# Modulation weight blocks loaded through GpSimd's queue instead of SyncE's, in a two-layer hybrid decoder

## The chip, the cores and the metric

The kernel runs on one core of one Trainium2 chip. A core has five engines with a queue of instructions each: TensorE (PE in the profile, its weight loads PEld), VectorE (DVE), ScalarE (ACT), GpSimd (POOL) and SyncE (SP). SyncE computes nothing; it issues DMAs. GpSimd computes and can issue DMAs too. Each queue is worked off in order: an instruction that waits holds up all that is behind it in its own queue. The metric is device time in microseconds (us) of one execution.

## The reference

Two layers over a residual stream of 1024 positions by 1024 channels, all float32. Each layer is:

```python
mod = c_act @ ada_w[l] + ada_b[l]            # c_act = silu(c): one row of 1024, ada_w[l]: 1024 x 6144
shift_m, scale_m, gate_m, shift_f, scale_f, gate_f = split(mod, 6)
h = rms_norm(x, g_pre_mix[l]) * (1 + scale_m) + shift_m
q, k, v, u = split(h @ w_in[l] + b_in[l])    # 512, 128, 128, 512 columns
attn = window_attention(rotary(q), rotary(k), v, sinks[l])   # window 128, 8 heads, 2 key heads
pool = pool_mixer(u, pool_w[l], pool_scale[l])
x = x + gate_m * rms_norm(concat(attn, pool) @ w_out[l], g_post_mix[l])
h = rms_norm(x, g_pre_ffn[l]) * (1 + scale_f) + shift_f
x = x + gate_f * rms_norm((silu(h @ w_gate[l]) * (h @ w_up[l])) @ w_down[l], g_post_ffn[l])
```

The change concerns the first line, the modulation: a product of one row with a matrix of 1024 x 6144 in each layer, 24 MB of weights that are read once and used for a single row.

## The kernel before

**The large products.** The sequence is worked in two halves of 512 positions. Every float32 product is made of three passes on TensorE: each operand is split into a high part (`hi`, written by ScalarE, L215) and a low part (`lo`, the rest, written by VectorE, L216), and `mm3` multiplies high by high (L255), high by low (L258) and low by high (L259). Weights arrive in `raw` (L225, issued by SyncE), are split, and are used at once. So TensorE depends at each step of a product on a DMA, on ScalarE and on VectorE.

**The modulation.** It is not done on TensorE as a matrix product. `ada_sum` takes blocks of 512 columns. Of a block it loads the eight pieces of 128 x 512 (256 KB each) one after another into the tile `ar` (L297), and VectorE multiplies each by a column of `c_act` and adds it into `ada` (L287 for the first piece, L289 for the seven others). `ar` has two buffers, so a piece can only be loaded once the sum of the piece two places earlier has freed its buffer. What is left in `ada` is one partial sum per partition; TensorE adds them up over the partitions with a few small matmuls (in `ada_pair`, `ada_gate` and `ada_columns`). `ada_pair` gives scale and shift, `ada_gate` a gate row, `ada_columns` scale and shift of the next layer's attention.

There are 20 such blocks, 160 loads. Eight blocks belong to each layer: two for the gate of attention, four for scale and shift of channel mixing and two for the gate of channel mixing. Four more, worked in layer 0's channel mixing, are scale and shift of layer 1's attention. (Layer 0's own shift and scale of attention are loaded in another way at the start and are not touched.)

**The order of the work.** The program is written as Python generators that are stepped against each other: `run(stream, steps, (other, n))` steps a main stream and lets others keep pace. The blocks of the modulation are a side stream (`side`). The stage in which it runs densest is this one, in each layer:

```python
run(out0, 2 * KD, (side, 4 * ADA), (att, 16))
```

`out0` is the output projection of half 0 (16 steps, `natural_proj`), `att` is the attention of half 1, and `side` works up to four blocks of the modulation meanwhile. A sum of the modulation is also tied behind the last split before it (`after(ins, recent["split"])`), so that it comes after that on VectorE.

From this program a scheduler makes the fixed order of each engine's queue. It weighs instructions by its own estimates of durations, those of the DMAs by the engine that issues them among them. So an edit of the issuing engine can also move instructions in queues that the edit doesn't name.

**What else stands in GpSimd's queue.** Set-up at the start, the zero fill of the value tiles of attention (`vz`, L752 and L760), the left margin of the pooling tiles (`uT`, L723 and L728, `halo`, L725) and the zeroed keys ahead of block 0 (`sa`, L782). One DMA is issued by GpSimd already: the load of the positions (L187).

**What else uses `ar`.** The rows of a gate (L441 and L442, stored by L448), the sums of the up projection (L1015) and the residual (L583), all issued by SyncE.

Of the kernel before, what the change touches and what calls it, by code (L numbers as in the profile page):

```python
# [65 lines left out]
def hybrid_decoder_kernel(  # L66
# [22 lines left out]
    nc = tc.nc  # L89
# [25 lines left out]
    def t_(tag, shape, dt=F32):  # L115
        if tag in SMALL:
            return small.tile(shape, dt, tag=tag, name=tag, bufs=SMALL[tag])
        if tag in SHARED:
            return sb.tile(shape, dt, tag=tag, name=tag, bufs=SHARED[tag])
        return now["pool"].tile(shape, dt, tag=tag, name=tag, bufs=REGIONS[now["name"]][tag])  # L120
# [92 lines left out]
    def split(hi, lo, src):  # L213

        nc.scalar.activation(hi, src, AF.Copy)  # L215
        recent["split"] = nc.vector.tensor_sub(lo, src, hi.bitcast(F32))  # L216
# [13 lines left out]
    def after(ins, prev):  # L230
        tc.add_manual_dep(
            ins.ins, prev.ins.name,
            mybir.DependencyInfo(mybir.DependencyClass.NoSync, mybir.DependencyReason.DATA),
            reason="order on the same engine",
        )
# [40 lines left out]
    def ada_sum(l, n0, got, whole=False):  # L276

        src = ada_w[l].rearrange("(p j) n -> p j n", j=KD)
        acc, ws = None, []
        for j in range(0, KD + 2, 2):
            for i, w in enumerate(ws, j - 2):
                if i == 0:
                    acc = t_("ada", [P, 512])
                    ins = nc.vector.tensor_scalar(acc, w, c_act[:, 0:1], None, op0=ALU.mult)  # L287
                else:
                    ins = nc.vector.scalar_tensor_tensor(  # L289
                        acc, w, c_act[:, i : i + 1], acc, op0=ALU.mult, op1=ALU.add  # L290
                    )
                after(ins, recent["split"])
            ws = []
            if j < KD:
                for i in (j, j + 1):
                    w = t_("ar", [P, 512])
                    nc.sync.dma_start(w, src[:, i, n0 : n0 + 512])  # L297
                    ws.append(w)
                yield
        if whole:  # L300
            got.append(acc)
        else:
            got += [t_("ph", [P, 512], F32R), t_("ph", [P, 512], F32R)]
            split(*got, acc)
        yield
# [156 lines left out]
    def ada_stream(jobs):  # L462

        for l, n0, close, *whole in jobs:
            got = []
            yield from ada_sum(l, n0, got, *whole)
            close(*got)
# [1105 lines left out]
```

## Time and profile before

| | |
|---|---|
| Time, median of 3 runs | 1915.66 us (1914.08 to 1919.38) |
| Profiled execution, its own time | 1912.51 us |
| Span from first to last instruction of it | 1910.7 us |
| TensorE busy | 1866.3 us (98%) |
| VectorE busy | 1545.1 us (81%) |
| ScalarE busy | 950.5 us (50%) |
| GpSimd busy | 26.8 us (1%) |
| Data moved by DMA | 341.86 MB, 179 GB/s over the span |
| of it by queue q1 (hardware_dynamic) | 340.17 MB |
| of it by queue q0 (software_dynamic) | under 0.01 MB, 32 packets |

The layers follow one another: attention and pooling of layer 0 to about 300 us, its channel mixing to about 950 us, layer 1's attention from about 985 to about 1250 us, then its channel mixing to the end. A row of a busy table gives, for a stretch of time, the busy time of each engine and in brackets the count of instructions, then the granted clock of TensorE as a share, the busy share of the DMA engines and GB/s. A row of a group gives the line in the code, the engine, the operation, the tiles written and read, and the count. A row of waits reads: who waited, for whom, how many us in total, how many times, the longest. "SPq" is SyncE's queue. The time of TensorE's matmuls is modelled and they overlap, so its busy share says less than the count of matmuls and the weight loads in a stretch.

### The profile page before, as it was taken

The page shows a single profiled execution, that of the slowest core. Times are in us where ns is not written, and L with a number is a line of the kernel's source. Part 1 is how long each engine was busy: PE and PEld are TensorE (multiplying, and loading weights), DVE is VectorE, ACT ScalarE, POOL GpSimd, SP SyncE. Part 2 cuts the span into 40 slices and gives each one's busy share as a digit, 9 for nine tenths or more (in the row PEclk, how much of TensorE's full clock was granted, in tenths as well). Part 3 has the DMA queues.
Part 4 walks back from the last instruction along what each step waited for, and adds up shares of the span by engine and source line. Part 5 has one row for each costly group of instructions (what it writes and reads, how often), then busy time and mean ns, then how long its engine had stood idle before and what let it go on. Part 6 is the DMA issues. An engine that isn't in the chain of part 4 may idle for free.

```text
span 1910.7 us, 26084 instructions
## 1 busy us (share of the span) xinstructions
PE 1866.3 (98%) x8978; PEld 1539.2 (81%) x8978; DVE 1545.1 (81%) x2898; ACT 950.5 (50%) x1789; POOL 26.8 (1%) x84
## 2 busy tenths in 40 slices
PE   6999999999999999999999989999999999999997
PEld 4887788888888888888888868888888887888886
DVE  5999886668898888788879998846889888877687
ACT  4876795653222223445548667845622222244452
POOL 1000000000000000000000000000000000000000
PEclk9999999999999999999999999999999999999999
DMA  9355563555655665944554464536654565574342
GB/s 324 115 155 153 163 226 122 186 177 183 204 179 189 208 207 178 323 137 145 183 168 128 133 183 165 177 110 208 215 188 150 198 209 202 197 252 150 115 152 102
DMA packets 227428, 341.86 MB, mean 179 GB/s; under 512 B 16952, under 2 KB 124360, under 8 KB 227296
## 3 DMA queue, kind: packets, MB, share of 16 engines
q1 hardware_dynamic: 227152, 340.17, 54.2%
q8 instruction: 70, 1.15, 0.2%
q14 instruction: 62, 0.51, 0.1%
q0 software_dynamic: 32, 0.00, 0.0%
q10 hardware_dynamic: 112, 0.04, 0.0%
HBM read 267.25 MB, written 72.89 MB: 178 GB/s over the span
## 4 chain that ended last, share of the span: by engine, by line
PE 79%; DVE 11%; DMA 5%; ACT 3%; issue 1%; SPq 0%; DVEq 0%; ACTq 0%
PE acc L255 24%; PE acc L258 24%; PE acc L259 24%; DMA ar<-in_ada_w_dram 2%; DVE lo L216 2%; DVE ada L289 2%; PE msc L851 1%; PE msc L519 1%; ACT hi L215 1%; DMA raw<-in_w_up_dram 1%; PE pv L255 1%; DVE ph L216 1%; DMA ar<-x 1%; DVE sb L816 1%; PE pv L258 1%
## 5 line engine op out<-in xcount | busy, mean ns | idle before, releaser
L215 ACT ACTIVATE hi<-raw 128x1024 fp32r<-128x1024 f32 (+1 forms) x388 | 332.4, 869 | 365.8 <-PE acc L258 196.2
L216 DVE TENSOR_TENSOR lo<-raw,hi 128x1024 fp32r<-128x1024 f32 (+1 forms) x388 | 380.0, 986 | 123.6 <-ACT hi L215 122.8
L255 PE MATMUL acc<-t,hi 128*128 128x512 f32 x704 | 274.6, 390 | 1.5 <-ACT hi L215 1.5
L258 PE MATMUL acc<-t,hi 128*128 128x512 f32 x704 | 274.0, 389 | 0.0
L259 PE MATMUL acc<-t,lo 128*128 128x512 f32 x704 | 271.9, 389 | 0.0
L255 PE MATMUL acc<-bh,hi 128*128 128x512 f32 x520 | 202.8, 390 | 0.0
L259 PE MATMUL acc<-bh,lo 128*128 128x512 f32 x520 | 202.4, 389 | 0.0
L255 PE MATMUL acc<-hT,hi 128*128 128x512 f32 x480 | 189.7, 395 | 0.6 <-DVE fn L638 0.6
L258 PE MATMUL acc<-hT,hi 128*128 128x512 f32 x480 | 188.4, 392 | 0.0
L259 PE MATMUL acc<-hT,lo 128*128 128x512 f32 x480 | 187.7, 392 | 0.0
L1107 DVE TENSOR_TENSOR fn<-acc,fn 128x512 f32<-128x512 f32 x220 | 150.2, 683 | 37.4 <-PE acc L259 37.4
L255 PEld LDWEIGHTS acc<-t,hi 128*128 128x128 f32 x704 | 132.2, 188 | 30.8 <-ACT hi L215 3.9
L259 PEld LDWEIGHTS acc<-t,lo 128*128 128x128 f32 x704 | 132.2, 188 | 29.0 <-DVE lo L216 1.5
L258 PEld LDWEIGHTS acc<-t,hi 128*128 128x128 f32 x704 | 132.2, 188 | 27.2
L258 PE MATMUL acc<-ph,hi 128*128 128x512 f32 x320 | 124.6, 389 | 0.0
L1043 ACT ACTIVATE fn<-fn 128x512 f32<-128x512 f32 x44 | 27.8, 633 | 180.3 <-DVE fn L1107 180.3
L289 DVE SCALAR_TENSOR_TENSOR ada<-ar,c_act,ada 128x512 f32<-128x512 f32 x140 | 104.6, 747 | 12.0 <-DMA ar<-in_ada_w_dram 11.0
L259 PEld LDWEIGHTS acc<-bh,lo 128*128 128x128 f32 x520 | 97.6, 188 | 20.4
L255 PEld LDWEIGHTS acc<-bh,hi 128*128 128x128 f32 x520 | 97.6, 188 | 20.0
L255 PEld LDWEIGHTS acc<-hT,hi 128*128 128x128 f32 x480 | 90.2, 188 | 18.9 <-DVE fn L638 1.4
L259 PEld LDWEIGHTS acc<-hT,lo 128*128 128x128 f32 x480 | 90.1, 188 | 18.2
L255 PE MATMUL acc<-hi 128*128 128x512 f32 x256 | 101.1, 400 | 2.8 <-DVE fn L638 1.6
(315 smaller groups left out, 3834.6 us busy)
## 6 DMA issues: line engine op xcount, KB each, us to landing
ar<-in_ada_w_dram SPq DMA_DIRECT2D x160, 256.0 KB
raw<-in_w_gate_dram SPq DMA_DIRECT2D x44, 512.0 KB
raw<-in_w_up_dram SPq DMA_DIRECT2D x44, 512.0 KB
raw<-in_w_in_dram SPq DMA_DIRECT2D x80, 256.0 KB
raw<-keeps SPq DMA_DIRECT2D x40, 512.0 KB
keeps<-fn SPq DMA_DIRECT2D x66, 256.0 KB
two_b<-in_w_down_dram SPq DMA_DIRECT2D x30, 512.0 KB
raw<-keepa SPq DMA_DIRECT2D x25, 512.0 KB
```

Source lines behind the costliest of these rows:

```text
L215: nc.scalar.activation(hi, src, AF.Copy)
L216: recent["split"] = nc.vector.tensor_sub(lo, src, hi.bitcast(F32))
L255: ins = nc.tensor.matmul(dst, lh, rh, start=first, stop=False)
L258: nc.tensor.matmul(dst, lh, rl, start=False, stop=False)
L259: return nc.tensor.matmul(dst, ll, rh, start=False, stop=last)
L289: ins = nc.vector.scalar_tensor_tensor(acc, w, c_act[:, i : i + 1], acc, op0=ALU.mult, op1=ALU.add)
L519: ins = nc.tensor.transpose(bank[:, t * P : (t + 1) * P], src[t], ident)
L816: nc.vector.tensor_tensor_reduce(out=s[:, ii, :], in0=bank[:, ii * 2 * P : (ii + 1) * 2 * P], in1=mask[:, min(blk, 1), :], scale=SCALE, sc ...
L851: nc.tensor.transpose(bank[:, i * P : (i + 1) * P], s[:, ii, ck * P : (ck + 1) * P], ident)
L1043: nc.scalar.activation(g, g, AF.Silu)
L1107: nc.vector.tensor_add(halves_of(dst)[m], bank, halves_of(src)[m])
```

## The change

One word of code: the 160 loads of `ada_sum` are issued by GpSimd.

```diff
@@ -294,7 +294,7 @@
             if j < KD:
                 for i in (j, j + 1):
                     w = t_("ar", [P, 512])
-                    nc.sync.dma_start(w, src[:, i, n0 : n0 + 512])
+                    nc.gpsimd.dma_start(w, src[:, i, n0 : n0 + 512])
                     ws.append(w)
                 yield
```

Shape, count, buffers and users of the loads stay as they are. The queues do not. SyncE's queue during the output projection of layer 0, before: weight loads of the projection (L225) and modulation loads (L297) alternate.

```order
L225 DMA raw<-in_w_out_dram 64x512 x6
L297 DMA ar<-in_ada_w_dram 128x512 x8
L225 DMA raw<-in_w_out_dram 64x512
L297 DMA ar<-in_ada_w_dram 128x512
L225 DMA raw<-in_w_out_dram 64x512
L297 DMA ar<-in_ada_w_dram 128x512
L225 DMA raw<-in_w_out_dram 128x512 x2
L297 DMA ar<-in_ada_w_dram 128x512
L225 DMA raw<-in_w_out_dram 128x512
L297 DMA ar<-in_ada_w_dram 128x512 x3
```

The same place in SyncE's queue with the change:

```order
L448 DMA gate<-ar 1x512
L457 DMA G<-gate 128x1024
L225 DMA raw<-in_w_out_dram 128x512
L225 DMA raw<-in_w_out_dram 64x512 x8
L225 DMA raw<-in_w_out_dram 128x512 x4
L225 DMA raw<-in_w_out_dram 64x512 x8
L225 DMA raw<-in_w_in_dram 128x512 x2
L546 DMA cfa<-in_x_dram 128x1024 x2
```

The weight loads of the projection now follow each other without a modulation load between them.

GpSimd's queue from the first part of attention to the end of the attention of layer 0, with the change (before, it held the same casts and copies and no L297):

```order
L297 DMA ar<-in_ada_w_dram 128x512 x7
L752 CAST vz<-vz_zero 128x64 x2
L297 DMA ar<-in_ada_w_dram 128x512 x4
L752 CAST vz<-vz_zero 128x64 x2
L297 DMA ar<-in_ada_w_dram 128x512 x4
L752 CAST vz<-vz_zero 128x64 x2
L297 DMA ar<-in_ada_w_dram 128x512 x20
L728 COPY uT<-halo 128x16
L297 DMA ar<-in_ada_w_dram 128x512 x4
L752 CAST vz<-vz_zero 128x64 x4
```

The zero fills of `vz` and the margin copy of `uT` now stand between loads that wait for a buffer.

VectorE's queue early in the output projection of layer 0, a piece of the difference (L289 are the sums of the modulation, L216 splits, L816 scores, L795 a split of queries):

```order
-L289 SCALAR_TENSOR_TENSOR ada<-ar,c_act,ada 128x512
 L216 TENSOR_TENSOR uT<-cfa,hi 128x512
-L216 TENSOR_TENSOR lo<-raw,hi 128x512
-L816 ISA sb,st<-msc,mask 128x256
-L816 ISA st 128x1
-L289 SCALAR_TENSOR_TENSOR ada<-ar,c_act,ada 128x512
-L816 ISA sb,st<-msc,mask 128x256
-L816 ISA st 128x1
+L289 SCALAR_TENSOR_TENSOR ada<-ar,c_act,ada 128x512
+L216 TENSOR_TENSOR lo<-raw,hi 128x512
 L216 TENSOR_TENSOR uT<-cfa,hi 128x512
 L289 SCALAR_TENSOR_TENSOR ada<-ar,c_act,ada 128x512
```

A sum that stood ahead of a split now stands behind it, and the scores between two sums have gone elsewhere; the number of instructions between the first and the last sum of the stage stays nearly the same.

## The prediction

> **What bounds the kernel now.** I read the page's busy shares first, then TensorE by stretches, then the chain of waits inside the weak stretches.
>
> ```profile
> span 1910.7 us, 26084 instructions
> PE 1866.3 (98%) x8978; PEld 1539.2 (81%) x8978; DVE 1545.1 (81%) x2898; ACT 950.5 (50%) x1789; POOL 26.8 (1%) x84
> ```
>
> TensorE seems full, but its busy time is modelled. The table of busy time by stretch says more, by the count of matmuls (the x behind PE) and by the weight loads (PEld).
>
> ```profile
> core 0: us, PE busy (x) PEld busy (x) DVE busy (x) ACT busy (x) POOL busy (x), PEclk, DMA share, GB/s
> 150.00:175.00 25.00, 21.84 (x115) 17.06 (x115) 24.17 (x63) 15.75 (x37) 0.42 (x2) 1.00 0.54 148
> 175.00:200.00 25.00, 23.47 (x118) 18.15 (x117) 23.57 (x61) 14.92 (x37) 0.00 (x0) 1.00 0.72 210
> 600.00:625.00 25.00, 25.00 (x112) 20.72 (x111) 21.90 (x30) 7.10 (x8) 0.00 (x0) 1.00 0.57 196
> 1100.00:1125.00 25.00, 22.26 (x110) 17.61 (x109) 23.05 (x67) 15.42 (x35) 0.00 (x0) 1.00 0.67 194
> 1125.00:1150.00 25.00, 22.25 (x104) 16.24 (x103) 21.35 (x56) 15.38 (x38) 0.73 (x1) 0.93 0.67 201
> ```
>
> In channel mixing (600 to 625 us) TensorE loads weights 20.72 us of 25 and is the bound. In the two stretches in which half 0's output projection runs beside half 1's attention (150 to 216 us in layer 0, 1098 to 1144 us in layer 1) it loads 16 to 18 us, while VectorE is full. These are the stretches in which the modulation's blocks stream densest. Their ring, for the whole of each stretch:
>
> ```profile
> 160.00:216.00 56.00, 51.31 (x258) 39.99 (x257) 51.69 (x136) 34.79 (x87) 0.77 (x3) 1.00 0.65 190
> 1098.00:1144.00 46.00, 40.52 (x193) 31.13 (x192) 42.50 (x111) 28.55 (x69) 1.65 (x3) 0.96 0.62 178
> ...
> L297 SPq DMA_DIRECT2D ar<-in_ada_w_dram x26: 327/328/519, 160.3 to 213.1; - x26
> L289 DVE SCALAR_TENSOR_TENSOR ada<-ar,c_act,ada x24: 742/752/832, 159.5 to 214.1; 128x512 f32<-128x512 f32 x24
>   DMA ar<-in_ada_w_dram: 3.3, 9
> ...
> L297 SPq DMA_DIRECT2D ar<-in_ada_w_dram x22: 327/328/440, 1098.4 to 1140.5; - x22
>   DMA ar<-in_ada_w_dram: 3.3, 6
> ```
>
> 26 loads go through the two buffers of `ar` between 160.3 and 213.1 us: 13 rounds of 4.1 us. In layer 1 there are 22, so 11 rounds of 3.8 us. The chain of waits, followed back inside these stretches, shows what a round is made of (start, us, what):
>
> ```profile
> by line: DMA ar<-in_ada_w_dram 48.0%; DVE ada L289 23.4%; DVE lo L216 9.4%; PE acc L258 4.6%; issue 3.6%; PE acc L259 3.6%; DVE sb L816 2.7%; DVE ph L216 2.3%; DVE qkv L707 2.3%; DVE ada L287 1.8%; DVE hi L795 1.4%; DVE hi L769 1.3%; PE msc
> 160.31 2.69 DMA ar<-in_ada_w_dram
> 163.10 0.83 DVE ada L289
> 164.59 0.76 DVE ada L289
> 165.37 2.78 DMA ar<-in_ada_w_dram
> 168.18 0.75 DVE ada L289
> 176.15 3.72 DMA ar<-in_ada_w_dram
> 179.96 0.75 DVE ada L289
> 184.71 3.28 DMA ar<-in_ada_w_dram
> ...
> 1110.94 3.83 DMA ar<-in_ada_w_dram
> 1116.29 0.60 DVE lo L216
> 1122.27 4.30 DMA ar<-in_ada_w_dram
> 1128.71 3.82 DMA ar<-in_ada_w_dram
> ```
>
> A sum (0.75 us) frees a buffer, SP issues the next load 0.02 us later, it lands after 2.7 to 4.3 us, and VectorE, in order, sums at once. Some 3.4 us and 0.75 us make the round of 4.1 us. VectorE waits openly only 3.3 us in each stretch, because other work fills the round almost exactly: load and VectorE are balanced. SP does not delay these loads, since it already stands waiting at them.
>
> **The change, part by part.** It adds no byte and no instruction of work. 160 issues of 256 KB leave SP's queue and stand in POOL's. The only rows for the two kinds of issue:
>
> ```profile
> L297 SPq DMA_DIRECT2D ar<-in_ada_w_dram x160: 327/328/1384, 50.4 to 1559.0; - x160
> L187 POOL DMA_DIRECT2D pos_i<-in_positions_dram x1: 1071/1071/1071, 3.3 to 3.3; - x1
> DMA to landing us min/median/max: 7.3/7.3/7.3
> ```
>
> 1. *Latency in the ring.* POOL's issue takes 1.071 us, SP's 0.328 us: 0.743 us more in every round, since nothing covers it there. 24 rounds x 0.743 = +17.8 us. VectorE's order is fixed and VectorE feeds a starved TensorE, so I let all of it through. Bounds: POOL's one DMA took 7.3 us to land, cold and beside a saturated start; against the mean of the seven chain loads above, 3.49 us, that is +3.8 us a round or +91 us. Downward, a queue of its own spares a load the weight loads ahead of it in SP's one queue. If each landed like the fastest row, 2.69 us, issue included, a round would lose 0.8 us, but only until VectorE's own work binds: it is idle 56.00 - 51.69 = 4.3 us and 46.00 - 42.50 = 3.5 us, so -7.8 us at most. I take +0.743, the nearer, because the fastest row plus 0.743 is 3.43 us, which only full relief from queueing would bring down to today's mean.
>
> The Trainium skill speaks against this size: "DMA: Bandwidth & Descriptors", section "Anatomy of one DMA — SWDGE (gpsimd) path", fits a GpSimd DMA as 2.0 us plus bytes over 436 GB/s, an estimate of 2.6 us for 256 KB. By it a round would shrink rather than grow, and the sum would be that of the second rival below. No row here shows a warm GpSimd load, so the trace can't decide.
>
> 2. *The rest of the run.*
>
> ```profile
> DVE ada L289 <- DMA ar<-in_ada_w_dram: 11.0, 23, 1.4
> SPq L297 <- DVE ada L289: 92.1, 77, 6.4
>   ACT hi L215: 3.7, 4
> ...
> 457.08 1.13 SPq L297 DMA_DIRECT2D ar<-in_ada_w_dram  x2
> 482.68 0.74 DVE L289 SCALAR_TENSOR_TENSOR ada<-ar,c_act,ada 128x512 f32<-128x512 f32 x1
> ```
>
> Of VectorE's 23 waits for a block, 9 + 6 lie in the two stretches and 8 outside. Two loads of a round overlap, so 8 / 2 x 0.743 = +3.0 us. In channel mixing a load has time (issued at 457.08, summed at 482.68 us), and TensorE's 20.72 us of weight loads bind: nothing there; if that cover were gone, the 0.743 us would come once a pair there too.
>
> 3. *SP freed.* SP stands over 92 us at L297, and weight loads queue behind it. But the row of ScalarE (who waited for the weight loads of L225) says that only 3.7 us of ScalarE's time, in 4 waits, hung on them. I take half, -1.9 us; bounds 0 and -3.7.
>
> 4. *VectorE's order.* The scheduler sets the sums later at the head of each stretch, by about three instructions of 0.60 us (a split, above). That is a lead once per stretch, not per round, because afterwards as many instructions lie between two sums as before: 2 x 1.8 = -3.6 us. Bounds: 0, and the whole again.
>
> 5. *POOL's own work* (26.8 us in all) now queues behind loads that wait. I cost it at nothing: the casts of `vz` stand between the same loads at whose time they ran before. What that is worth if wrong is a rival.
>
> Sum: 17.8 + 3.0 - 1.9 - 3.6 = +15.3 us. The profiled execution took 1912.51 us, 1.8 us more than its span; that makes 1927.8 us. It was 3.2 us faster than the median of the three runs, 1915.66 us, so I give 1931 us.
>
> **The rivals.**
>
> *A wait taken away (faster).* A load no longer stands behind weight loads in SP's queue, nor they behind it. For it: the chain's loads spread from 2.69 to 4.30 us although all are 256 KB. Against: they still share the same 16 DMA engines, 0.62 to 0.65 busy in these stretches. It decides when POOL's extra cost is below the relief, about 0.5 us. Price: -7.8 us of VectorE's idle time and up to -3.7 us of SP's: 1904 to 1909 us.
>
> *Hidden anyway.* Extra cost and relief cancel: the mean of 3.49 us is already the fastest row plus 0.8 us. Then terms 1 and 2 fall to some +5 us and terms 3 and 4 take them back: 1911 to 1920 us.
>
> *VectorE holds up the issue.* A POOL issue could be blocked while certain VectorE instructions run, and VectorE is full here.
>
> ```profile
> L841 DVE TENSOR_SCALAR sb<-sb,st 128x256 f32<-128x256 f32 x7 | 2.1, 350 | 0.0
> L287 DVE TENSOR_SCALAR ada<-ar,c_act 128x512 f32<-128x512 f32 x3 | 1.4, 478 | 0.0
> ```
>
> If each round met one of either, 24 x (0.350 + 0.478) = +20 us on top: 1951 us. Against: these are 3.5 us of a stretch of 56. The Trainium skill has the mechanism: "SBUF — State Buffer", section "Who interferes with whom", says that copies and tensor_scalar in a two-port mode lock GpSimd out, and that descriptor generation starves meanwhile. The trace before cannot show it.
>
> *POOL as the bound.* POOL waits at a load for up to a round, 4.1 us, with casts of `vz` behind it, and ScalarE and VectorE finish the values of attention only after them. Seven groups of casts stand between loads, by half a round each: 7 x 2.05 = +14 us on top, 1945 us.
>
> ```profile
> POOL vz L752 <- PE pv L259: 167.3, 10, 27.2
>   DVE vz L756: 2.0, 2
> ```
>
> For it: VectorE did wait 2.0 us for `vz`. Against: POOL itself waits for TensorE there, 167.3 us, not for its place in the queue.
>
> **How the numbers follow.** The ring's latency 0.55, hidden 0.14, a wait taken away 0.13, VectorE holding up the issue 0.12, POOL 0.06. The likeliest one's own range is 1921 to 1943 us (extra cost 0.3 to 1.25 us a round). The range, 1908 to 1952 us, takes in part of the faster case below and VectorE's hold-up above, and leaves out landings as slow as the cold one. A difference under 0.3%, 5.7 us, cannot be told from none here. Slower: 0.55 + 0.12 + 0.06, less 0.02 of the first that stays inside, is 0.71. The same: 0.16. Faster: 0.13.
>
> **What would show it.** Right: L297 on POOL at about 1.07 us each; the two stretches 8 to 10 us and 7 to 8 us longer; VectorE's wait at L289 for the load growing from 11.0 us to over 25; DMA `ar` growing in the chain; the other stages as before. Wrong: chain loads of 3 us or less and a shorter stretch (a wait taken away); POOL issues far over 1.1 us (held up by VectorE); ScalarE or VectorE waiting for POOL's `vz` (POOL as the bound). If the stretches grow but the end does not, TensorE was not starved by VectorE and term 1 is misread.

## The result, and the profile after

The changed kernel takes 1945.99 us (median of 4 runs, 1944.72 to 1950.58), the kernel before 1914.87 us in the same comparison. The ratio is 1.0166, 95% interval 1.0146 to 1.0185. It is slower by 31.1 us, about twice the +15.3 us of the forecast's sum, and the time lies inside the stated range (1908 to 1952 us). It does so by luck in part: it is above the 1921 to 1943 us that the forecast gave its own mechanism, and the upper end of the range was there for VectorE holding up the issues, of which the runs show no sign. The profiled execution took 1945.2 us, 32.7 us more than the profiled one before.

The head of the page of the kernel after:

```profile
span 1943.1 us, 26195 instructions
...
PE 1878.2 (97%) x8978; PEld 1545.0 (80%) x8978; DVE 1544.7 (79%) x2898; ACT 950.7 (49%) x1789; POOL 114.1 (6%) x244
```

VectorE does the same 2898 instructions in the same time (1545.1 us before, 1544.7 us now). So what it lost is idle time: span less busy time was 365.6 us before and is 398.4 us now, 32.8 us more, while the span grew by 32.4 us. One row explains nearly all of it. These are VectorE's waits for a modulation block in the whole run after (in all, times, longest):

```profile
DVE ada L289 <- DMA ar<-in_ada_w_dram: 42.9, 38, 4.1
...
DVE ada L287 <- DMA ar<-in_ada_w_dram: 2.4, 2, 2.2
```

Before they were 11.0 us in 23 waits; now 45.3 us in 40, 34.3 us more. The place is the one the forecast named. Where along the run it happens is another matter. The same row for five consecutive parts of the run before (0 to 157, 157 to 230, 230 to 985, 985 to 1094, 1094 to 1160 us: layer 0 up to the dense stretch, its dense stretch, the channel mixing, layer 1 up to its dense stretch, that stretch):

```profile
DVE ada L289 <- DMA ar<-in_ada_w_dram: 1.1, 2, 0.8
DVE ada L289 <- DMA ar<-in_ada_w_dram: 3.3, 9, 0.7
DVE ada L289 <- DMA ar<-in_ada_w_dram: 2.8, 5, 1.4
DVE ada L289 <- DMA ar<-in_ada_w_dram: 0.5, 1, 0.5
DVE ada L289 <- DMA ar<-in_ada_w_dram: 3.3, 6, 1.1
```

And for the same parts after (0 to 163, 163 to 247, 247 to 1004, 1004 to 1119, 1119 to 1195 us):

```profile
DVE ada L289 <- DMA ar<-in_ada_w_dram: 4.8, 4, 2.6
DVE ada L289 <- DMA ar<-in_ada_w_dram: 10.3, 11, 2.5
DVE ada L289 <- DMA ar<-in_ada_w_dram: 10.2, 7, 3.8
DVE ada L289 <- DMA ar<-in_ada_w_dram: 9.1, 6, 4.1
DVE ada L289 <- DMA ar<-in_ada_w_dram: 8.5, 10, 2.7
```

The two dense stretches gained 7.0 and 5.2 us (7.4 in layer 1 with the row at L287), but the parts outside gained 19.7 us. Waits of 2.6 and 3.8 us stand there, which no fixed price of a GpSimd issue explains. (The longest, 4.1 us, is a case of its own, told under the run that clears GpSimd.)

The loads of the two stretches themselves (first and last issue, and the time from issue to landing) and, below them, the busy times in the two stretches after:

```profile
L297 POOL DMA_DIRECT2D ar<-in_ada_w_dram x26: 539/539/542, 166.3 to 226.0; - x26
...
DMA to landing us min/median/max: 2.8/3.0/6.3
...
L297 POOL DMA_DIRECT2D ar<-in_ada_w_dram x22: 539/539/569, 1124.6 to 1172.9; - x22
...
DMA to landing us min/median/max: 2.9/3.0/5.4
```

```profile
166.00:229.00 63.00, 53.01 (x251) 39.68 (x249) 50.73 (x133) 33.02 (x78) 15.02 (x29) 0.97 0.59 176
1124.50:1178.00 53.50, 44.15 (x193) 32.26 (x192) 42.24 (x112) 28.96 (x69) 12.97 (x25) 0.94 0.57 171
```

Of the two stretches VectorE was idle 4.3 and 3.5 us before and is idle 12.3 and 11.3 us now, while TensorE's weight loads stay nearly the same (39.99 and 31.13 us before): TensorE has the same work and gets it later.

The 26 loads of layer 0 were issued from 160.3 to 213.1 us before, over 52.8 us, and take 59.7 us now: +6.9 us, 0.53 us a round. The 22 of layer 1 took 42.1 us and take 48.3: +6.2 us, 0.56 us a round. The two issue times also tell how far each point of the program was behind: 6.0 us at the head of the first stretch, 12.9 at its last load, 26.2 at the head of the second, 32.4 at its last load. So 13.1 us came inside the stretches, 6.0 us ahead of the first and 13.3 us between them.

An issue takes 0.539 us, not the 1.071 us of the one row there was before. What a round is made of shows in the chain of waits after (start, us, what), here at one of the slow loads of layer 0's stretch:

```profile
193.22 0.75 DVE ada L289
...
194.26 5.59 DMA ar<-in_ada_w_dram
```

The sum ends at 193.97 and GpSimd starts its issue at 194.26, 0.29 us later (SyncE: 0.03). The fastest landing of all 160 loads is 2.80 us; before it was 2.57 us, by the semaphore updates in the trace. And this load took 5.59 us. At its end the busy table shows the DMA engines full, VectorE idle and TensorE short of work:

```profile
198.00:200.00 2.00, 1.24 (x6) 0.67 (x4) 0.05 (x1) 0.98 (x3) 0.00 (x0) 1.00 1.08 288
```

What SyncE did meanwhile, from its timeline after:

```profile
193.06 4.34 SPq L225 DMA_DIRECT2D raw<-in_w_out_dram  x7
```

Seven weight loads were sent one behind the other, from 193.06 to 197.40 us, with the modulation load of 194.26 among them. The same part of the work on SyncE's timeline before:

```profile
188.80 0.33 SPq L297 DMA_DIRECT2D ar<-in_ada_w_dram  x1
189.18 1.75 SPq L225 DMA_DIRECT2D raw<-in_w_out_dram  x3
192.13 0.33 SPq L297 DMA_DIRECT2D ar<-in_ada_w_dram  x1
192.51 0.47 SPq L225 DMA_DIRECT2D raw<-in_w_out_dram  x1
```

In one queue SyncE stands at a modulation load until its buffer is free, and the weight loads behind it stand too. They come out in ones and threes, each behind a modulation load. The forecast counted that standing as 92 us of lost SyncE time. It may be what kept the weight loads out of the way; that is one of the explanations to be tried.

### The profile page after: what moved, and what is told of

Same layout as the page of the kernel before. It is cut to its first block, busy times and chain, and to the rows that moved or that the text cites. A ratio compares the mean times of both kernels' runs of the same rounds, so it can differ in the third digit from the quotient of the medians.

```text
span 1943.1 us, 26195 instructions
## 1 busy us (share of the span) xinstructions
PE 1878.2 (97%) x8978; PEld 1545.0 (80%) x8978; DVE 1544.7 (79%) x2898; ACT 950.7 (49%) x1789; POOL 114.1 (6%) x244
## 4 chain that ended last, share of the span: by engine, by line
PE 74%; DVE 11%; DMA 8%; issue 3%; ACT 3%; POOL 0%; SPq 0%; DVEq 0%; ACTq 0%; POOLq 0%
PE acc L255 23%; PE acc L258 22%; PE acc L259 22%; DMA ar<-in_ada_w_dram 5%; DVE lo L216 2%; DMA raw<-in_w_up_dram 1%; DVE ada L289 1%; PE msc L851 1%; PE msc L519 1%; ACT hi L215 1%; DVE fn L1107 1%; PE pv L255 1%; PE pv L258 1%; DMA ar<-x 1%; PE pv L259 1%
## 5 line engine op out<-in xcount | busy, mean ns | idle before, releaser
L216 DVE TENSOR_TENSOR lo<-raw,hi 128x1024 fp32r<-128x1024 f32 (+1 forms) x388 | 379.9, 986 | 117.6 <-ACT hi L215 116.8
L297 POOL DMA_DIRECT2D ar<-in_ada_w_dram x160 | 86.5, 541 | 1200.3 <-DVE ada L289 362.0
L289 DVE SCALAR_TENSOR_TENSOR ada<-ar,c_act,ada 128x512 f32<-128x512 f32 x140 | 104.7, 748 | 43.6 <-DMA ar<-in_ada_w_dram 42.9
L258 PE MATMUL acc<-lo,hi 128*128 128x512 f32 x256 | 103.1, 407 | 2.3 <-DVE lo L216 2.2
```

The lines of the kernel that those rows point to most:

```text
L258: nc.tensor.matmul(dst, lh, rl, start=False, stop=False)
L289: ins = nc.vector.scalar_tensor_tensor(acc, w, c_act[:, i : i + 1], acc, op0=ALU.mult, op1=ALU.add)
L297: nc.gpsimd.dma_start(w, src[:, i, n0 : n0 + 512])
```

## The experiments

Three explanations were open for the half that the forecast missed. *Latency:* GpSimd starts later and its loads land later, and that costs in more places than the dense stretches. *Overtaking:* weight loads that SyncE no longer holds back get ahead of a modulation load and slow its landing. *GpSimd's own work:* copies and casts, waiting for other engines, stand ahead of a load. A fourth, the new order of VectorE's instructions, is a rival to all of them.

**Which loads.** One line sends either the 64 loads of channel mixing's shift and scale (the dense stretches, and the last few ahead of them) or the other 96 by GpSimd:

```diff
-                    nc.sync.dma_start(w, src[:, i, n0 : n0 + 512])
+                    (nc.gpsimd if 3 * D <= n0 < 5 * D else nc.sync).dma_start(w, src[:, i, n0 : n0 + 512])
```

> Only the 64 loads of the blocks for channel mixing's scale and shift (the two dense stretches, and the same columns elsewhere) go by GpSimd, the other 96 by SyncE. All work is done. The forecast's terms 1 and 4 put +14 us here: 1929 us. By the trace after, in which the stretches from 160 to 250 us and from 1125 us on grew by 10 and 6 us: +16 us, 1931 us. If the cost is everywhere alike, by count of loads, 64/160 of 31 = +12 us.

> The counterpart: the 96 other loads by GpSimd, the 64 of the dense stretches by SyncE. All work is done. The forecast's term 2 put +3 us here: 1918 us. By the trace after, in which the first part of each layer's attention grew by 5 to 7 us and channel mixing by 2: +14 us, 1929 us. By count of loads 96/160 of 31 = +19 us. If the two parts add, this and the run before sum to +31 us.

Measured: the 64 alone 1936.34 us against 1914.14 us, ratio 1.0115 (1.0100 to 1.0130), +22.2 us. The other 96 alone 1919.48 us, ratio 1.0023 (1.0013 to 1.0033), +5.3 us. VectorE's waits for a block, with the 64 on GpSimd:

```profile
DVE ada L289 <- DMA ar<-in_ada_w_dram: 25.3, 31, 2.3
```

and with the other 96:

```profile
DVE ada L289 <- DMA ar<-in_ada_w_dram: 26.0, 31, 3.7
```

The two add to 27.5 of the 31.1 us, so the parts are nearly independent. Each moves the waits by about 15 us, but the same waiting costs 22 us in one kernel and 5 us in the other. Half of the second kernel's lies in layer 0's channel mixing (233 to 986 us), where VectorE's waits are:

```profile
DVE lo L216 <- ACT hi L215: 49.5, 43, 3.7
DVE ada L289 <- DMA ar<-in_ada_w_dram: 11.1, 8, 3.7
```

In the same part before (230 to 985 us) the wait for a block was 2.8 us, and the one for ScalarE:

```profile
DVE lo L216 <- ACT hi L215: 54.7, 46, 3.7
```

There 8.3 us more of the one wait are paid back by 5.2 us less of the other: VectorE has idle time to give. The forecast's claim that the time is made by the loads of the dense stretches holds, but they cost 22.2 us and not the 14 us of its terms 1 and 4. My reading by the trace after, +14 us for the rest, was wrong: what grew ahead of the dense stretches comes in part only when both groups are moved.

**Is it overtaking?** First the weight traffic itself was taken away. The output projection's blocks, which run beside the dense stretches, are loaded for 16 partitions only:

```diff
-            return ((ALLP, None, w_out[l, k * P : (k + 1) * P, cs]),)
+            return ((slice(0, 16), None, w_out[l, k * P : k * P + 16, cs]),)
...
-                wh, wl = weight(*wsrc(k, nh))
+                wh, wl = weight(*wsrc(k, nh), sub_=G[:, 0:512])
```

> Modulation loads by SyncE, as before the change. Of the output projection's weight blocks (the loads that stand beside the modulation's in the two dense stretches) only 16 of 128 partitions are loaded, and the split reads another tile of the same size in their place: seven eighths of these bytes are left out, all of the computing is still done. This is the control of the next run. Contention matters little with everything in one queue: 1905 to 1914 us, up to 8 us below the kernel before (VectorE waited 8.1 us there for loads that took over 3.5 us).

> The same with the modulation loads by GpSimd, as after the change; the same seven eighths of the output projection's weight bytes are left out. If the modulation's loads are slowed by weight loads that SyncE, no longer held back, sends in bursts: in the dense stretches VectorE's waits at loads over 3.5 us grew from 3.6 to 15.3 us, so this run comes out about 12 us closer to its control than the changed kernel to its own, +19 us, near 1928 us. If the price is one of latency for each round, whatever else is moved: +31 us over its control still, near 1940 us.

Measured: 1915.96 us by SyncE, 1938.77 us by GpSimd, +22.8 us in place of +31.1. The loads of layer 0's dense stretch by SyncE, and then by GpSimd:

```profile
L297 SPq DMA_DIRECT2D ar<-in_ada_w_dram x26: 327/328/382, 160.6 to 214.1; - x26
```

```profile
L297 POOL DMA_DIRECT2D ar<-in_ada_w_dram x26: 539/539/539, 166.9 to 224.1; - x26
...
DMA to landing us min/median/max: 2.8/2.9/5.4
```

The stretch grows from 53.5 to 57.2 us: +3.7 us, 0.28 us a round, where it was +6.9 us with the weights' bytes. In layer 1 it grows from 43.1 to 46.4 us: +3.3 us in place of +6.2. So about half of the stretches' growth needs the weight traffic beside it, and half does not. Over the whole run 8 us went, not the 12 us expected: the input projection's loads were left as they were, and the 6.3 us at the head of the stretch (160.6 to 166.9) remain. VectorE's waits for blocks remain too for the most part; over the whole run by GpSimd, against 10.2 us by SyncE:

```profile
DVE ada L289 <- DMA ar<-in_ada_w_dram: 37.1, 36, 5.4
```

Then the ring got a third buffer, with everything else at work (a mask in bf16 and smaller tiles make the room, in both):

```diff
-    SHARED = dict(hT=8, fn=4, raw=2, hi=3, lo=3, sa=2, sb=2, ar=2, ada=1, ph=3, G=1)
+    SHARED = dict(hT=8, fn=4, raw=2, hi=3, lo=3, sa=2, sb=2, ar=3, ada=1, ph=3, G=1)
```

> Modulation loads by SyncE, with three buffers in their ring instead of two (room for it from a mask in bf16, half as many halo buffers, a one-column zero and no tile of its own for the rows). All work is done. Control of the next run. VectorE's 11.0 us of waits for a load shrink to about half: 1905 to 1912 us.

> The same with the modulation loads by GpSimd. With three buffers a load has more than one sum's time in hand, about 2 us more a round, so both a later start (0.26 us), a longer landing (0.26 us) and most of the slow ones are covered: at most +8 us over the control, 1910 to 1918 us. If the ring is not where the time goes (order of the instructions, a port that VectorE and GpSimd share): +25 us or more over the control.

Measured: 1912.66 us by SyncE (ratio to the kernel before 0.9993, 0.9983 to 1.0002), 1928.09 us by GpSimd, +15.4 us. By SyncE that is just above the 1905 to 1912 us that I expected. VectorE's waits there:

```profile
DVE ada L291 <- DMA ar<-in_ada_w_dram: 1.2, 5, 0.3
```

By GpSimd, with the landing times, a piece of the chain, and SyncE's timeline at that place:

```profile
DVE ada L291 <- DMA ar<-in_ada_w_dram: 21.0, 23, 3.2
```

```profile
DMA to landing us min/median/max: 2.8/3.5/7.5
```

```profile
184.85 4.84 DMA ar<-in_ada_w_dram
...
191.78 6.33 DMA ar<-in_ada_w_dram
```

```profile
187.86 4.36 SPq L227 DMA_DIRECT2D raw<-in_w_out_dram  x7
```

With a third buffer half of the 31 us is indeed gone, as it should be if a start that is 0.27 us late and a landing a few tenths longer are covered. What stays in the chain are landings of 4.8 and 6.3 us, again beside seven weight loads in a row. I had expected at most +8 us; what a third buffer does not cover is worth more than that, be it slow landings or the order of the instructions.

Last, two queues without GpSimd in the ring: the modulation on SyncE, the projections' weight loads on GpSimd.

```diff
-            nc.sync.dma_start(dst, src)
+            nc.gpsimd.dma_start(dst, src)
```

> The other way round: modulation loads by SyncE as before the change, but the weight loads of the projections by GpSimd. All work is done. The two kinds of load stand in two queues, as after the change, while the ring of the modulation has SyncE's start of 0.03 us and landing of 2.6 us. If two queues are what costs (weight loads go past a modulation load and slow its landing): +8 to +15 us, 1922 to 1930 us. If GpSimd's latency in the ring is what costs: within 5 us of the kernel before, 1910 to 1920 us, because weights are loaded a block ahead.

Measured: 1928.07 us against 1914.06 us, ratio 1.0071 (1.0056 to 1.0086), +14.0 us. The modulation's loads of layer 0's dense stretch, VectorE's waits for blocks, and a wait at the start of the program:

```profile
L297 SPq DMA_DIRECT2D ar<-in_ada_w_dram x26: 327/328/573, 164.9 to 219.4; - x26
```

```profile
DVE ada L289 <- DMA ar<-in_ada_w_dram: 19.0, 23, 1.9
...
DVE ar L346 <- DMA cfb<-in_ada_w_dram: 3.8, 1, 3.8
```

And who waited for the weight loads that GpSimd now issues:

```profile
  ACT hi L215: 0.2, 1
```

The ring has SyncE's latency here, nobody waits for GpSimd's weight loads to speak of (3.7 us before), and yet VectorE waits 8.0 us longer for its blocks (11.0 to 19.0). So two queues cost without GpSimd's latency, unless the new order of VectorE's instructions, which this edit brings too, has a share in it. It is not the whole +14.0 us: 3.8 us are a wait for the first loads of the program, which this edit moves as well, and the dense stretch is only 1.7 us longer (54.5 against 52.8).

**Do bursts come from the tiles?** SyncE's weight tiles hold four blocks and come free together. Outside channel mixing they were replaced by six tiles of one block and one of two (channel mixing keeps its two tiles of four):

```diff
-    SHARED = dict(hT=8, fn=4, raw=2, hi=3, lo=3, sa=2, sb=2, ar=2, ada=1, ph=3, G=1)
+    SHARED = dict(hT=8, fn=4, hi=3, lo=3, sa=2, sb=2, ar=2, ada=1, ph=3, G=1)
...
-        mix=dict(cfa=2, cfb=2, qkv=6, bqkv=1, uT=4, pt=2, vz=5, rt=1, qT=1, pth=2, pwh=1, pwl=1),
+        mix=dict(raw=6, rawb=1, cfa=2, cfb=2, qkv=6, bqkv=1, uT=4, pt=2, vz=5, rt=1, qT=1, pth=2, pwh=1, pwl=1),
```

> Modulation loads by SyncE. The two tiles of four weight blocks each that SyncE loads into outside channel mixing are replaced by six tiles of one block and one of two, so that a buffer comes free, and is loaded, one block at a time and not four. All work is done. Control of the next run: 1908 to 1920 us.

> The same with the modulation loads by GpSimd. If bursts of four weight blocks ahead of a modulation load make its landing long (5 to 6 us): most of the slow landings go, and the distance to the control is +15 us or less, near 1930 us. If single weight loads beside it slow it as much, or if the price is latency: +25 to +31 us over the control.

Measured: 1977.83 us by SyncE and 1995.88 us by GpSimd, +18.1 us, between the two expectations. The control is itself 64 us slower than the kernel before, so the pair says little of time. It falls behind along the whole run: by 13 us at the start of layer 0's channel mixing, 27 at its end, 54 at the start of layer 1's; why is not isolated. The waits by GpSimd say more (by SyncE they were 11.6 us):

```profile
DVE ada L294 <- DMA ar<-in_ada_w_dram: 42.0, 42, 3.7
```

```profile
DMA to landing us min/median/max: 2.8/3.4/7.2
```

They are as long as in the changed kernel (42.9 us), with landings up to 7.2 us. Letting blocks free one at a time does not stop the slow landings, so the four-block tiles are not what makes them.

**GpSimd's own work.** Its memsets went to VectorE, its halo copies and casts to ScalarE:

```diff
-            nc.gpsimd.tensor_copy(v[:, 1, :], vz_zero)
+            nc.scalar.activation(v[:, 1, :], vz_zero, AF.Copy)
...
-                nc.gpsimd.tensor_copy(halo, ut[:, T : T + HALO])
+                nc.scalar.activation(halo, ut[:, T : T + HALO], AF.Copy)
```

> The changed kernel with GpSimd's own work taken off it: its memsets go to VectorE, its halo copies and the casts of vz to ScalarE. All work is done. In the trace of the changed kernel VectorE waited 8.3 us for four loads that GpSimd issued 0.8 to 2.7 us after their buffer was free, because its own copies and casts, waiting for other engines, stood ahead. If that is so: 6 to 8 us less than the changed kernel, about 1938 us. If those loads are late for another reason, or the work costs as much on the other engines: 1944 us or more.

Measured: 1943.33 us, ratio 1.0146 (1.0129 to 1.0163). Against 1.0166 for the changed kernel that is at most a small gain; the intervals overlap. One of the late loads is even as late as ever. VectorE's sum that frees its buffer, and GpSimd's next issue:

```profile
1056.31 0.48 DVE L287 TENSOR_SCALAR ada<-ar,c_act 128x512 f32<-128x512 f32 x1
```

```profile
1059.53 1.08 POOL L297 DMA_DIRECT2D ar<-in_ada_w_dram  x2 [8.70 <-DVE pt L956]
```

The sum ends at 1056.79 and GpSimd, with nothing else to do, issues at 1059.53, 2.74 us later instead of 0.29. In the changed kernel a halo copy stood ahead of this load, and I took it for the cause. It is not. The row names VectorE's `pt`, but that is only VectorE's last signal before the start. It is the 107th load of the modulation, and it starts 2.74 us after its sum in the changed kernel as well, and in the two kernels by GpSimd with few weight bytes and with tiles of one block. In the last of these the sum ends at 1089.19 us, VectorE itself stands idle from 1090.46 to 1091.83 us, and still the load does not start until:

```profile
1091.92 1.08 POOL L302 DMA_DIRECT2D ar<-in_ada_w_dram  x2 [9.04 <-issue]
```

So neither GpSimd's own work nor VectorE's instructions account for it; what does stays open. In the changed kernel this one load makes the longest wait, 4.1 us, and with GpSimd cleared VectorE waits 6.0 us for it, so that it hides in part what clearing GpSimd may have gained.

**The order of the instructions.** Each load was split by partitions between the two queues, once with the large piece on GpSimd and once with the small one. PE, VectorE and ScalarE have the same order of instructions in both kernels.

```diff
-                    nc.sync.dma_start(w, src[:, i, n0 : n0 + 512])
+                    nc.gpsimd.dma_start(w[0:112], src[0:112, i, n0 : n0 + 512]); nc.sync.dma_start(w[112:P], src[112:P, i, n0 : n0 + 512])
```

> Every modulation load is split: partitions 0 to 111 go by GpSimd, 112 to 127 by SyncE. SyncE therefore waits at every load as before the change, and its weight loads stay behind it; GpSimd's latency stands in the ring as after the change. All work is done. Ring latency (GpSimd starts 0.29 us instead of 0.03 us after the buffer is free, and the load lands 0.26 us later): still slower, 24 rounds x 0.5 us = +12 us and some more outside the stretches, 1927 to 1935 us. If the weight loads that SyncE no longer holds back are what makes up the other half of the +31 us: clearly below the changed kernel, about 1930 us. If they are not: 1940 us or more, as the changed kernel.

> The mirror of the run before: partitions 0 to 111 by SyncE, 112 to 127 by GpSimd. The engines' order of instructions is the same in both, so that only the queue of the large and the small piece differs. All work is done. Ring latency: the small piece is issued 0.26 us late but has less to move, so at most +6 us: 1912 to 1921 us. If GpSimd's own work ahead of a load (casts and copies that wait for TensorE) is what costs: the small piece is held by it just as the whole load was, 1925 us or more. If the new order of the instructions costs the 31 us: both kernels of this pair come out alike.

Measured: 1939.06 us with the large piece on GpSimd (ratio 1.0129, 1.0114 to 1.0144; +24.9 us), 1926.26 us with the small one (1.0069, 1.0053 to 1.0086; +12.1 us). At one order the queue of the large piece makes 12.8 us, so the order alone is not the cause; what share it has was not isolated. With SyncE held back at every load, as before the change, the cost is 6 us below the changed kernel's: nearer to the second expectation (1940 us) than to the first (1930 us). This does not speak for overtaking as all of the missing half. It is no clean test of it either: SyncE is let go as soon as the buffer is free, and GpSimd starts the large piece 0.27 us later, so the weight loads behind the small piece can still get ahead. The small piece cost more than the 6 us expected. Moreover the split makes a new wait in both kernels. GpSimd's waits in the second:

```profile
  DMA ar<-in_ada_w_dram: 36.4, 11
```

The second writer of a tile waits for the first one's loads, which neither kernel before or after does.

What the first of the pair does show is that SyncE's standing does not bring fast landings back. Those of its large pieces:

```profile
DMA to landing us min/median/max: 2.7/3.3/6.4
```

**Where slow landings come from.** The semaphore updates in the traces give the landing of every load, SyncE's too. VectorE's 11.0 us of waits before contain 7.5 us at loads that took over 3.5 us; of the 45.3 us after, 37.5 us stand at such loads. Before, 50 of 160 loads were that slow, after it is 59; the difference lies in the slowest. Of the 160 loads this many took over 4.8 us, a bound set here:

| Kernel | Queues | Over 4.8 us |
|---|---|---|
| before; few weight bytes, tiles of one block, three buffers, by SyncE | one | 6; 5, 6, 16 |
| after; few weight bytes, tiles of one block, three buffers, by GpSimd | two | 22; 20, 22, 43 |
| GpSimd's own work taken off | two | 29 |
| modulation by SyncE, weights by GpSimd | two | 14 |
| split, large piece by GpSimd (that piece), SyncE standing at every load | two | 30 |

While a load over 4.8 us was under way the DMA engines were 0.90 busy on average before and 0.91 after; for loads up to 3.5 us it was 0.63 and 0.53. So the slow landings fall where the DMA engines are full, and in each pair there are more of them with two queues than with one. In the split kernel, which sends each load as two DMAs, SyncE's standing does not keep them away. Why two queues make more of them than one is not shown.

## Why the prediction was right in sign and half in size

**Term 1, latency in the ring (+17.8 us), and term 4, order (-3.6 us).** Together 14.2 us for the dense stretches, where 13.1 us came between their first and last loads. For these two pieces of the run the number is right, by luck, and its make-up is not. The 0.743 us of a slower issue was a cold row: an issue takes 0.539 us, and lies inside the landing time. In its place stand a start 0.27 us later and a landing at best 0.23 us longer (2.80 against 2.57 us). Without most of the weights' bytes the round grows by 0.28 us, and by as much again with them; whether they slow the landings or only take away the slack was not told apart. The order's credit never came. At the end of layer 0's block there was a debt instead, in VectorE's waits from 163 to 247 us:

```profile
DVE sb L816 <- PE msc L814: 3.7, 3, 1.9
DVE colp L399 <- PE msc L395: 1.6, 1, 1.6
DVE ph L216 <- ACT ph L215: 1.1, 1, 1.1
```

In the same part before, only the first of them stood, at 1.1 us. The last sum's followers (its split, the transposes, the addition at L399) now seem to come with little other work left to cover them. The forecast's own range has a slip as well: with 0.3 to 1.25 us a round also in term 2 it is 1919 to 1945 us, not 1921 to 1943, and the measured time is outside of both.

**Term 2, the rest of the run (+3.0 us): the step that failed.** I counted the 8 waits that VectorE already had outside the stretches and charged each half an issue. The sign that I gave, the other stages as before, failed: 19.3 us came there by the issue times (6.0 ahead of the first stretch, 13.3 between the two). Of the 13.3, 3.8 us belong to the end of layer 0's block (VectorE's first instruction of channel mixing, at L1073, starts at 283.6 us before and 300.3 after), 1.7 to channel mixing (the last L571 on `sa` starts at 979.2 and 997.6) and 7.8 to the part ahead of the second stretch, 4.1 of them the wait for the one late load. So some 14 us lie ahead of the two stretches, where the forecast had 3. There the loads had a little slack before, and the term put them at nothing: a load that now takes 4 to 6 us where it took 3 uses up the slack and becomes a wait of its own, of up to 2.6 us ahead of the first stretch. In channel mixing such waits reach 3.8 us and cost little. By loads and not by place, the 96 outside the pair cost 5.3 us when they alone are moved, near the term, and the pair's 64 cost 22.2 us, 8 us over terms 1 and 4; the remaining 3.6 us come only where both are moved.

**Term 3, SyncE freed (-1.9 us).** The row of ScalarE's waits for weight loads of L225 did fall, from 3.7 us to 0.7:

```profile
  ACT hi L215: 0.7, 2
```
That wait went; what it was worth in time was not measured. Naming what is queued behind a wait was right; what I didn't ask is which transfers would then be under way beside the modulation's.

**Term 5, GpSimd's own work (0).** About right, by the run without that work: 1943.33 against 1945.99 us, with intervals that overlap.

**The rivals.** All issues of the kernel after:

```profile
L297 POOL DMA_DIRECT2D ar<-in_ada_w_dram x160: 539/539/613, 45.5 to 1591.5; - x160
```

*A wait taken away* had the queue right and the sign wrong: with two queues the modulation's loads landed later and not earlier. *Hidden anyway* needed landings that make up for the price; the minimum alone is longer. *VectorE holds up the issue:* no sign of it in the issues themselves, which take 0.539 us, with a maximum of 0.613 us over all 160; and the one load that starts 2.7 us late does so with VectorE idle too. *GpSimd as the bound:* in layer 0 VectorE waited 2.0 us for `vz` before and 1.2 us after, ScalarE 1.7 us both times, and its work is not what makes the time. The Trainium skill's fit for a GpSimd load ("DMA: Bandwidth & Descriptors", section "Anatomy of one DMA — SWDGE (gpsimd) path"), an estimate of 2.6 us for 256 KB, lies near the 2.8 us of the fastest landing here and says nothing of the 3.0 to 7.5 us that loads took in the runs by GpSimd. That a round would shrink by it did not come true: a load by SyncE landed in 2.57 us at best and started sooner.

**What the 31 us are, as far as the runs settle it.** A third buffer takes 16 us away and leaves 15; leaving out seven eighths of the output projection's bytes takes 8. Two queues without GpSimd's latency cost 14, of which 3.8 are at the start. So the price is hardly GpSimd's latency alone: slow landings beside a second queue have a share, though each of these three figures holds other things too. That weight loads overtake because SyncE no longer stands is not shown, since with SyncE standing the slow landings stayed. The split isn't settled either, because a slow landing only hurts where latency has used up the slack, and the order's share wasn't isolated.

## What to carry to other kernels

A second queue is not only relief: before a load is moved to one, list what is queued behind it and ask which transfers the moved load will then share the DMA engines with. Where a ring of two buffers is balanced to a few tenths of a microsecond, price a move by the slack of every load in the run, not by the waits that already show, since a load with 1 us of slack becomes a wait as soon as its landing grows by two. Here a third buffer took half of the price away and left the other half.

## What the runs showed of the hardware that was not expected

- GpSimd's issue of a 256 KB load took 0.539 us (at most 0.613 over all 160), against 1.071 us for the single cold one of 7.3 us landing; it began 0.29 us after the sum that freed the buffer (within 0.02 us in 130 of the 158 loads that follow the first two), SyncE's 0.03 us.
- The 160 loads of 256 KB landed in 2.57 to 5.63 us (median 3.14) by SyncE, in one queue with the weight loads, and in 2.80 to 6.53 us (median 3.12) by GpSimd, beside SyncE's queue. The median hardly differs; loads over 4.8 us went from 6 to 22.
- A third buffer with SyncE cut VectorE's waits for blocks from 11.0 to 1.2 us and the time by nothing that can be measured (ratio 0.9993): so in that kernel those 11 us were idle time that cost nothing to speak of (its smaller tiles may hide a little), while the waits for blocks, grown by 34 us, went with 31 us of time.
- One load, the 107th by GpSimd, started 2.74 us after its buffer was free, in four kernels, with and without GpSimd's own work, with VectorE busy all along or idle for 1.37 us of it; no row shows why.
